# Mixture of experts, sorted on the chip by token count, every second expert in blocks of 64 tokens

## Chip, cores and metric

One core of a Trainium2 chip. The metric is the device time of one execution in microseconds, the median of several runs.

## The reference, cut to what matters

Two transformer blocks over 512 tokens of width 1024, all in float32. The change is in the second block's mixture of experts: 32 experts, each token goes to its four best.

```
logits = xt @ w_router + b_router
top_vals, top_idx = top_k(logits, 4);  gates = softmax(top_vals)
for each expert e, for the tokens xb that chose it:
    hgu = xb @ w_up_gate[e] + b_up_gate[e]            # 1024 -> 2048
    x_glu = min(hgu[:, :1024], 7);  x_lin = clip(hgu[:, 1024:], -7, 7)
    hact = x_glu * sigmoid(1.702 * x_glu) * (x_lin + 1)
    y = hact @ w_down[e] + b_down[e]                  # 1024 -> 1024
    out[token] += gate * y
```

`setup_inputs` draws fixed inputs, so each expert's count is fixed too.

## The kernel before

Float32 products are made of three passes over float32r parts: a value is split into a high part (ScalarE, L185) and a rest (VectorE, L188), and high x high, high x low and low x high are summed in PSUM (L165 issues every product).

The experts are a pipeline of steps (`moe`, L1769; `expert_step`, L1594). Step e runs, in 12 slots of one weight chunk (1 MB) each: four slots gate(e), four slots linear(e), four slots down(e-1). Each slot has 12 products of 128x128 by 128x512: two blocks of 128 rows of the weight, two PSUM banks, three parts. A block holds up to 128 tokens and is the stationary operand; the weights move. Beside the products stand, at fixed slots: evacuation and scatter of the outputs of e-2 (`evac`, L1641), transposes and split of the activations of e-1 (`tact`, `eact`), SiLU and clamp of e (`gate`, `act`), transposes and split of the gathered rows of e+1 (`tx`, `ex`), and the one-hot matrix, token table and row gather of e+2 (`gather_onehot`, `gather_table`, `gather_rows`, L1490 to L1538). Each engine works in the written order.

Weights come by SP's queue (`m_load`, L1547) in packets of 4 KB into 11 buffers of 1 MB (`mraw`), are split two chunks ahead (`m_ahead`, L1560, `m_la` = 2) into a ring of three hi/lo pairs (`mhl`, L1751), and PE releases a pair when its last product is done. PSUM is a rotation of eight banks (`ps`, L274 and L148). Bias rows enter as a first product of a selecting tile (`E4`) with all experts' biases (`BD`).

An expert with more than 128 tokens doesn't fit one block. Place 14 (`TWO`) has a second block in its step; `plan` finds on the chip the first expert from place 5 on that overflows and `swap` exchanges it with expert 14, before their weights are loaded by a run-time index (`order`). Blocks beyond that run in a loop after the steps (`tc.For_i`, L1854), each for itself. Every block runs the same instructions, whether it holds 16 tokens or 128.

The router (L1312) makes counts and ranks (`posm`), gates (`R`) and the first block before the steps begin.

Of the kernel before, what the change touches and what calls it, by code (L numbers as in the profile page):

```python
# [10 lines left out]
F32 = mybir.dt.float32  # L11
# [9 lines left out]
S = 512  # L21
D = 1024
# [6 lines left out]
TWO = 14  # L29
SWAP = 5  # L30
# [3 lines left out]
             ("cw2", 44), ("cb", 44), ("sbq", 1), ("sbk", 1), ("brt", 1),  # L34
             ("b_ada", 48)]
ROW_PARTS = [("mq_r", 32), ("mk_r", 32), ("rq", 64), ("rk", 64), ("gng", 512), ("gnb", 512)]
CST_PARTS = [("ident", 128), ("trin", 128), ("slow", 128), ("negm", 128), ("inv16", 16), ("inv32", 32),
             ("i32", 32), ("i128", 128), ("e4", 32), ("ule", 32), ("tok4", 4)]
# [12 lines left out]
COFF, CN = offsets(CST_PARTS)  # L51


def constants():
    p = np.arange(P)
    f = np.float32
    out = np.zeros((P, CN), f)

    def put(n, a):
        out[:, COFF[n][0]:COFF[n][1]] = a  # L60
# [9 lines left out]
    put("e4", (p[:, None] % 32) == np.arange(32)[None])  # L70
# [5 lines left out]
    return out, np.ascontiguousarray(dec.transpose(1, 0, 2))  # L76
# [7 lines left out]
def host_arrays(inp):  # L84
    g = {k: np.asarray(v) for k, v in inp.items()}
    one64 = np.ones(64, np.float32)
    one32 = np.ones(32, np.float32)
    cw = g["conv_w"].reshape(3, 2 * DFF)

    def hg(v):  # L90
# [10 lines left out]
        brt=np.concatenate([g["b_router_2"].reshape(-1), one32, one64])[:, None], b_ada=col(g["b_ada"]),  # L101
# [33 lines left out]
class Kernel:  # L135
# [25 lines left out]
    def cc(self, n):  # L161
        return self.cst[:, COFF[n][0]:COFF[n][1]]
# [1149 lines left out]
    def router(self, cr, right):  # L1312
# [41 lines left out]
        idf = rp.tile([P, NT, 4], F32, name="idf")  # L1354
        nc.vector.tensor_copy(idf, i8[:, :, 0:4])
        oh = rp.tile([P, NT * 4, NE], F32, name="oh")
        nc.vector.tensor_tensor(oh, idf.rearrange("p t r -> p (t r)")[:, :, None].to_broadcast([P, NT * 4, NE]),
                                self.cc("i32")[:, None, :].to_broadcast([P, NT * 4, NE]), op=OP.is_equal)
# [3 lines left out]
        nc.vector.memset(cm[:, 0, :], 0.0)  # L1362
        for t in range(NT):
            nc.vector.tensor_tensor(cm[:, t + 1, :], cm[:, t, :], M[:, t, :], op=OP.add)
        pp = self.ps()
        f = "p t e -> p (t e)"
        self.mm(pp[:, 0:NT * NE], self.cc("slow"), M.rearrange(f), True, False)
        self.mm(pp[:, 0:NT * NE], self.ones, cm[:, 0:NT, :].rearrange(f), False, True)
        pc = self.ps()
        self.mm(pc[0:NE, 0:1], cm[:, NT, :], self.ones[:, 0:1], True, True)  # L1370
        self.warm(10)
        pos = rp.tile([P, NT, NE], F32, name="pos")
        nc.vector.scalar_tensor_tensor(pos, pp[:, 0:NT * NE].rearrange("p (t e) -> p t e", e=NE), 1.0, M, op0=OP.add,
                                       op1=OP.mult)
        nc.vector.tensor_scalar(self.posm, pos, -1.0, 1.0, op0=OP.mult, op1=OP.add)
        nc.scalar.activation(self.cnt, pc[0:NE, 0:1], AF.Copy)
# [6 lines left out]
        for t in range(NT):  # L1383
# [10 lines left out]
        tmp = rp.tile([P, NT * 4, NE], F32, name="tmp")  # L1394
        nc.vector.tensor_tensor(tmp, oh, g4.rearrange("p t r -> p (t r)")[:, :, None].to_broadcast([P, NT * 4, NE]),
                                op=OP.mult)
        nc.vector.tensor_reduce(out=self.R[:, :, :, 1], in_=tmp.rearrange("p (t r) e -> p t e r", r=4), axis=AX.X,
                                op=OP.add)
# [4 lines left out]
    def overflow_blocks(self, rp):  # L1403

        nc = self.nc
        self.nb = nb = rp.tile([NE, 4], F32, name="nb")
        for b in range(3):
            nc.vector.tensor_scalar(nb[:, b:b + 1], self.cnt, 128.0 * (b + 1), None, op0=OP.is_gt)
        nc.vector.tensor_reduce(out=nb[:, 3:4], in_=nb[:, 0:3], axis=AX.X, op=OP.add)

    def plan(self, rp):


        nc, nb = self.nc, self.nb
        i32, jc = self.cc("i32")[0:16, :], self.cc("tok4")[0:16, 0:1]
        ci = rp.tile([16, NE], F32, name="ci")
        df = rp.tile([16, NE], F32, name="df")
        le = rp.tile([16, NE], F32, name="le")
        q = rp.tile([16, 4], F32, name="q")
        X = rp.tile([16, 4], F32, name="X")  # L1420
        ts, tt = nc.vector.tensor_scalar, nc.vector.tensor_tensor
        mx, has, two, dd = [q[:, k:k + 1] for k in range(4)]

        def place(out, e, t):
            ts(t, e, two, dd, op0=OP.is_equal, op1=OP.mult)
            tt(out, e, t, op=OP.add)
            ts(t, e, float(TWO), dd, op0=OP.is_equal, op1=OP.mult)
            tt(out, out, t, op=OP.subtract)

        pc = self.ps()  # L1430
        self.mm(pc[0:16, 0:NE], nb[:, 0:1].to_broadcast([NE, 16]), self.cc("ident")[0:NE, 0:NE], True, True)
        ts(le, i32, -1.0, float(2 * NE), op0=OP.mult, op1=OP.add)
        tt(le, le, pc[0:16, 0:NE], op=OP.mult)
        nc.vector.tensor_reduce(out=mx, in_=le[:, SWAP:NE], axis=AX.X, op=OP.max)
        yield
        ts(has, mx, 0.0, None, op0=OP.is_gt)
        ts(two, mx, -1.0, float(2 * NE - TWO), op0=OP.mult, op1=OP.add)
        tt(two, two, has, op=OP.mult)
        ts(dd, two, -1.0, None, op0=OP.mult)
        ts(two, two, float(TWO), None, op0=OP.add)  # L1440
        yield
        place(df, i32, le)
        nc.vector.tensor_copy(self.order[:, 0:NE], df[0:1, :])
        nc.vector.tensor_copy(self.order[:, NE:NE + 1], two[0:1, :])
        yield
        pc = self.ps()
        self.mm(pc[0:16, 0:NE], nb[:, 3:4].to_broadcast([NE, 16]), self.cc("ule")[0:NE, :], True, True)
        ts(le, i32, two, has, op0=OP.is_ge, op1=OP.mult)
        tt(ci, pc[0:16, 0:NE], le, op=OP.subtract)
# [4 lines left out]
        nc.vector.tensor_reduce(out=X[:, 0:1], in_=le, axis=AX.X, op=OP.add)  # L1454
        ts(X[:, 0:1], X[:, 0:1], float(NE - 1), None, op0=OP.min)
# [4 lines left out]
        ts(X[:, 2:3], X[:, 0:1], two, has, op0=OP.is_equal, op1=OP.mult)  # L1460
        tt(X[:, 1:2], X[:, 1:2], X[:, 2:3], op=OP.add)
        ts(X[:, 1:2], X[:, 1:2], 128.0, 128.0, op0=OP.mult, op1=OP.add)
        yield
        place(X[:, 3:4], X[:, 0:1], mx)
        nc.vector.tensor_copy(X[:, 2:3], ci[:, NE - 1:NE])
        Xi = rp.tile([16, 4], I32, name="Xi")
# [8 lines left out]
    def swap(self, rp):

        nc = self.nc
        e = nc.values_load(self.order[0:1, NE:NE + 1], engines=[mybir.EngineType.DVE], min_val=SWAP, max_val=NE - 1)
        def at(x):
            return (self.posm[:, :, x].rearrange("p t o -> p (t o)"),  # L1480
                    self.R[:, :, x, :].rearrange("p t o c -> p (t o) c"),
                    self.E4[:, :, x].rearrange("p i o -> p (i o)"))

        w = (rp.tile([P, NT], F32, name="sw0"), rp.tile([P, NT, 2], F32, name="sw1"), rp.tile([P, 2], F32R, name="sw2"))
        a, b = at(bass.ds(e, 1)), at(slice(TWO, TWO + 1))
        for to, fro in ((w, a), (a, b), (b, w)):
            for x, y in zip(to, fro):
                nc.vector.tensor_copy(x, y)

    def gather_onehot(self, d):  # L1490

        nc = self.nc
        oh = d["oh"] = self.mo.tile([P, NT, P], F32, name="ohp")
        for t in range(NT):
            nc.scalar.activation(oh[:, t, :], self.cc("i128"), AF.Abs, bias=d["pos"](t))
        oh = oh.rearrange("p t r -> p (t r)")
        nc.scalar.activation(oh, oh, AF.Relu, scale=-1.0, bias=1.0)
# [62 lines left out]
    def m_ahead(self):  # L1560
        while self.m_i < min(len(self.m_seq), self.m_done + 1 + self.m_la):
# [3 lines left out]
            self.split(raw, hi, lo)  # L1565
# [20 lines left out]
    def hl_tile(self, nm, d):  # L1586
# [4 lines left out]
        p = self.mx if nm == "x" else self.ml  # L1591
        return (p.tile([P, 8, P], F32R, name=nm + "h"), p.tile([P, 8, P], F32R, name=nm + "l"))

    def expert_step(self, cur=(), prev=(), pp=(), nxt=(), extra=None):  # L1594


        nc = self.nc
# [440 lines left out]
```

## Time and profile before

| | us |
|---|---|
| median of 3 runs | 2331.49 (2329.19 to 2333.32) |
| the profiled execution | 2335.76 |
| its span, first to last instruction | 2333.5 |
| PE / VectorE / ScalarE with work in the span | 2289.0 / 1748.6 / 1470.8 |

PE, DVE, ACT, POOL and SP are TensorE, VectorE, ScalarE, GpSimd and SyncE. A busy engine is one with an instruction in work; products are pipelined, so the start of one to the start of the next tells more than the length of one. "PEclk" is the clock granted to TensorE as a share of full speed, "DMA" the mean busy share of the 16 DMA engines. A wait is put down to the engine whose signal came last. Times in the rows count from the first instruction.

### The profile page before, as it was taken

How to read it: one execution, taken by the hardware profiler on the slowest of the kernel's cores; microseconds unless marked ns; L12 is line 12 of the kernel's file. 1: busy time of each engine (PE TensorE's matmuls, PEld its weight loads, DVE VectorE, ACT ScalarE, POOL GpSimd, SP SyncE). 2: the span in 40 equal slices, each digit the busy share in tenths (PEclk: the TensorE clock that was granted, in tenths of full speed). 3: DMA queues.
4: the chain of work that ended last, by engine and by line, in shares of the span. 5: the costliest groups of instructions: out<-in, count | busy, mean ns of one | idle time of the engine just before them, and what ended most of it. 6: DMA issues, size and time to landing. Idle time of an engine off the chain costs nothing. (4 is left out here: it accounts for less than half of the span.)

```text
span 2333.5 us, 29383 instructions
## 1 busy us (share of the span) xinstructions
PE 2289.0 (98%) x10792; PEld 1870.6 (80%) x10792; DVE 1748.6 (75%) x2138; ACT 1470.8 (63%) x1829; POOL 197.0 (8%) x108
## 2 busy tenths in 40 slices
PE   9999999999999999989999999999999999999988
PEld 8875688888888777777888888888888888888877
DVE  6877775566557367568988898867788889898963
ACT  3676543334444348556777878766687777877764
POOL 0100000000000000020011111200111011111100
PEclk8999999999999999999999999999999999999999
DMA  9240434333233122559999999987999999999861
GB/s 330 83 139 10 140 104 128 116 109 109 100 110 100 45 91 73 176 181 318 350 351 356 356 348 365 332 293 268 325 362 356 357 349 355 357 348 355 295 229 62
DMA packets 184611, 538.45 MB, mean 231 GB/s; under 512 B 16277, under 2 KB 41397, under 8 KB 184272
## 3 DMA queue, kind: packets, MB, share of 16 engines
q1 hardware_dynamic: 170128, 508.08, 60.9%
q0 software_dynamic: 11792, 26.12, 4.0%
q10 hardware_dynamic: 2544, 2.34, 0.3%
q8 instruction: 86, 1.41, 0.2%
q14 instruction: 61, 0.50, 0.1%
HBM read 530.47 MB, written 23.59 MB: 237 GB/s over the span
## 5 line engine op out<-in xcount | busy, mean ns | idle before, releaser
L188 DVE TENSOR_TENSOR mlo<-mraw,mhi 128x2048 fp32r<-128x2048 f32 x389 | 884.0, 2286 | 170.4 <-ACT mhi L185 151.3
L185 ACT ACTIVATE mhi<-mraw 128x2048 fp32r<-128x2048 f32 x389 | 741.5, 1914 | 283.3 <-PE ps L165 274.3
L165 PE MATMUL ps<-mhi,xh 128*128 128x512 f32 x1024 | 405.9, 396 | 0.0
L165 PE MATMUL ps<-mhi,xl 128*128 128x512 f32 x1024 | 401.2, 392 | 2.1 <-DVE xl L1581 2.1
L165 PE MATMUL ps<-mlo,xh 128*128 128x512 f32 x1024 | 274.1, 389 | 0.0
L188 DVE TENSOR_TENSOR wlo<-raw,whi 128x1024 fp32r<-128x1024 f32 (+2 forms) x128 | 153.1, 1207 | 112.4 <-ACT whi L185 112.2
L165 PEld LDWEIGHTS ps<-mhi,xl 128*128 128x128 f32 x1024 | 193.1, 189 | 42.3 <-DVE xl L1581 2.5
L165 PEld LDWEIGHTS ps<-mlo,xh 128*128 128x128 f32 x1024 | 192.2, 188 | 40.5
L165 PEld LDWEIGHTS ps<-mhi,xh 128*128 128x128 f32 x1024 | 192.9, 188 | 39.1 <-ACT xh L1580 0.2
L185 ACT ACTIVATE whi<-raw 128x1024 fp32r<-128x1024 f32 (+2 forms) x128 | 132.3, 1043 | 132.7 <-PE ps L165 131.3
L165 PE MATMUL ps<-mhi,ah 128*128 128x512 f32 x512 | 206.3, 403 | 0.3 <-ACT ah L1583 0.3
L165 PE MATMUL ps<-mhi,al 128*128 128x512 f32 x512 | 201.0, 393 | 0.2 <-DVE al L1584 0.2
L165 PE MATMUL ps<-whi,hh 128*128 128x512 f32 (+1 forms) x464 | 184.8, 398 | 5.5 <-ACT hh L185 2.4
L165 PE MATMUL ps<-wlo,hh 128*128 128x512 f32 (+1 forms) x464 | 181.6, 391 | 2.2 <-DVE wlo L188 2.2
L165 PE MATMUL ps<-whi,hl 128*128 128x512 f32 (+1 forms) x464 | 180.8, 390 | 0.0
L165 PE MATMUL ps<-mlo,ah 128*128 128x512 f32 x512 | 137.9, 391 | 0.0
L165 PE MATMUL ps<-hh,whi 128*128 128x512 f32 x352 | 137.8, 392 | 0.0
L1536 POOL DMA_INDIRECT xg<-hn_d,ix x31 | 72.6, 2343 | 769.9 <-PE ps L165 647.2
L165 PE MATMUL ps<-hh,wlo 128*128 128x512 f32 x352 | 137.0, 389 | 0.0
L165 PE MATMUL ps<-hl,whi 128*128 128x512 f32 x352 | 136.9, 389 | 0.0
L165 PEld LDWEIGHTS ps<-mlo,ah 128*128 128x128 f32 x512 | 96.1, 188 | 21.2
L165 PEld LDWEIGHTS ps<-mhi,ah 128*128 128x128 f32 x512 | 96.3, 188 | 20.1 <-ACT ah L1583 0.7
(487 smaller groups left out, 3660.1 us busy)
## 6 DMA issues: line engine op xcount, KB each, us to landing
mraw<-in_w_ug SPq DMA_DIRECT2D x256, 1024.0 KB, 7.8
mraw<-in_w_dn SPq DMA_DIRECT2D x128, 1024.0 KB, 7.5
raw<-in_w_up SPq DMA_DIRECT2D x44, 512.0 KB, 3.5
raw<-in_w_in SPq DMA_DIRECT2D x40, 512.0 KB, 3.7
wa<-in_w_ada SPq DMA_DIRECT2D x12, 1024.0 KB, 10.0
raw<-in_w_ada SPq DMA_DIRECT2D x24, 512.0 KB, 4.5
raw<-in_w_down SPq DMA_DIRECT2D x22, 512.0 KB, 3.5
raw<-in_w_out SPq DMA_DIRECT2D x16, 512.0 KB, 4.8
```

Source lines behind the costliest of these rows:

```text
L165: self.nc.tensor.matmul(out, l, r, start=start, stop=stop, skip_group_check=True)
L185: self.nc.scalar.activation(hi, raw, AF.Copy)
L188: self.nc.vector.tensor_tensor(lo, raw, hi, op=OP.subtract)
L1536: nc.gpsimd.indirect_dma_start(out=d["xg"], out_offset=None, in_=self.hn_d, in_offset=bass.IndirectOffsetOnAxis(ap=ix, axis=0), bounds_che ...
```

## The change

The ranks, gates and one-hot tables are made a second time after a sort: places 0 to 2 keep experts 0 to 2, the other 29 experts are ordered by count, and the upper 15 and the lower 14 take turns. The weights' run-time index starts at place 3. Place 3 (the largest count) has the second block. Places 4, 6, ... 30 are small: capacity 64. A small block's stationary tile has the high parts of its 64 tokens in columns 0 to 63 and the low parts in 64 to 127, so that two products (with the high and the low part of the weight) make all four terms; rows r and r + 64 of the result belong to one token. They are added for the activations by products with a matrix of two stacked identities (`sum2`), which also transpose, and for the outputs by scattering both halves with addition, one DMA each. Rows of a small block are gathered as two half rows, to partitions r and r + 64.

Gate and linear are no longer separate: one up chunk is 128 rows of the weight by all 2048 columns, with four PSUM banks open for eight slots. A down chunk gives partition p the rows 2p and 2p + 1. Both are 8 KB per partition in one piece. The columns of the activations are therefore read from PSUM at every second place (`pairs`). The first chunks are split in halves (`m_cut`). One tile `xg` instead of two holds gathered rows. The outputs of e-2 are evacuated ahead of the step's first product instead of behind it. The swap is gone, the plan of the overflow loop comes later and counts against each place's capacity.

```diff
-TWO = 14
-SWAP = 5
+FIRST = 3
+BIG = 15
+TWO = FIRST
+SMALL = [p >= FIRST and (p - FIRST) % 2 == 1 for p in range(NE)]
+CAP = [256 if p == TWO else 64 if SMALL[p] else 128 for p in range(NE)]
...
+    def sort(self, rp):
+        ts(kc, self.cnt, 32.0, self.cc("key")[0:NE], op0=OP.mult, op1=OP.add)
+        ps = self.ps()
+        self.mm(ps[0:NE, 0:NE], kc.to_broadcast([NE, NE]), ident, True, True)
+        ts(G, ps[0:NE, 0:NE], kc, None, op0=OP.is_lt)
+        yield
...
+        self.choices(oh)
+        yield
+        tt(tmp, oh, pl[:, None, :].to_broadcast([P, NT * 4, NE]), op=OP.mult)
...
+        pp, pc = self.ranks(rp, M, cm)
+        self.set_ranks(pp, pc, t[:, 3 * NT * NE:4 * NT * NE].rearrange("p (t e) -> p t e", e=NE), M)
+        yield
+        self.gates(oh, tmp)
+        self.select(self.ob, self.cc("val"))
...
             hi, lo = [self.mhl.tile([P, 2 * D], F32R, name=n) for n in ("mhi", "mlo")]
-            self.split(raw, hi, lo)
+            n = 2 * D // self.m_cut
+            for c in range(self.m_cut):
+                cs = slice(c * n, (c + 1) * n)
+                self.split(raw[:, cs], hi[:, cs], lo[:, cs])
...
-                    mms(d, ((0, 0), (1, 0)), False)
+                    mms(d, 0, range(len(d[x])), False)
...
-                    mms(d, ((0, 1),), True)
+                    mms(d, 1, (0,), True)
...
+        def act(d):
+            if d.get("small"):
+                d["us"] = [self.ma.tile([P, D], F32, name="mg") for _ in range(2)]
+                for b in range(4):
+                    z = wide(d["us"][b // 2][:, b % 2 * 512:b % 2 * 512 + 512])
+                    if b % 2:
+                        nc.vector.tensor_copy(z, pairs(d.pop(("u", b))))
+                    else:
+                        nc.scalar.activation(z, pairs(d.pop(("u", b))), AF.Copy)
+                return
...
+            for r in (slice(0, 64), slice(64, P)) if d.get("small") else (slice(0, P),):
+                nc.gpsimd.indirect_dma_start(
...
+            ps = d["aps", b] = self.ps()
+            for k in range(8):
+                self.mm(ps[:, k * 64:k * 64 + 64], d["us"][b][:, k * P:(k + 1) * P], self.cc("sum2"), True, True)
...
+        slots = [((cur, "x", "u", 0, 4, c), no, no) for c in range(8)] + \
+                [((prev, "a", "d", 1, 2, c), no, no) for c in range(4)]
...
+        put(0, on(evac, pp))
+        put(1, on(tact, ta, 0), on(eact, ta, 0))
+        put(2, on(tact, ta, 1), on(eact, ta, 1))
+        put(8, on(gate, cur), on(act, cur))
+        put(9, on(tx, nxt, 0), on(ex, nxt, 0))
+        put(10, on(tx, nxt, 1), on(ex, nxt, 1))
...
-        for w, b in ((wu, 0), (wu, 1), (wd, 0)):
-            if w is not None:
-                s += [w[c * 256:(c + 1) * 256, b * D:(b + 1) * D].rearrange("(k p) n -> p k n", p=P) for c in range(4)]
+        if wu is not None:
+            s += [wu[c * P:(c + 1) * P, :].rearrange("(k p) n -> p k n", p=P) for c in range(8)]
+        if wd is not None:
+            s += [wd[c * 256:(c + 1) * 256, :].rearrange("(p k) n -> p k n", p=P) for c in range(4)]
```

## Rows read from the trace of the kernel before

**Rows 1.** The page, parts 1 and 2: busy us and share; busy tenths in 40 slices.
```profile
PE 2289.0 (98%) x10792; PEld 1870.6 (80%) x10792; DVE 1748.6 (75%) x2138; ACT 1470.8 (63%) x1829; POOL 197.0 (8%) x108
...
DMA  9240434333233122559999999987999999999861
```

**Rows 2.** Windows: us, then PE, PEld, DVE, ACT, POOL busy, PEclk, DMA share, GB/s.
```profile
1110.00:1500.00 390.00, 390.00 (x1846) 324.19 (x1845) 346.02 (x264) 305.28 (x270) 52.17 (x22) 1.00 0.98 355
...
1035.00:1040.00 5.00, 4.37 (x24) 3.47 (x23) 4.79 (x11) 4.32 (x7) 0.00 (x0) 1.00 0.58 199
...
1060.00:1065.00 5.00, 2.85 (x14) 2.13 (x13) 4.72 (x14) 2.88 (x3) 1.02 (x1) 0.86 0.91 333
```

**Rows 3.** Waits of the whole span: who waited for whom, us, times, longest us.
```profile
POOL xg L1536 <- PE ps L165: 647.2, 26, 31.0
...
ACT mhi L185 <- PE ps L165: 274.3, 303, 3.8
...
DVE mlo L188 <- DMA mraw<-in_w_ug: 17.0, 27, 1.3
```

**Rows 4.** Timeline of PE in one steady step: start us, length us, line, operation, tiles.
```profile
1704.39 0.63 PE L165 MATMUL ps<-BD,E 128*128 128x512 f32 x2
...
1707.62 0.39 PE L165 MATMUL ps<-mhi,xh 128*128 128x512 f32 x1
...
1710.34 0.39 PE L165 MATMUL ps<-mhi,xh 128*128 128x512 f32 x1
...
1719.00 0.95 PE L165 MATMUL ps<-R,ohp 128*128 128x2 f32 x8
1719.80 0.64 PE L181 MATMUL ps<-cst,xg 128*128 128x128 f32 x4
...
1720.19 0.48 PE L165 MATMUL ps<-mhi,ah 128*128 128x512 f32 x1
...
1741.31 0.63 PE L165 MATMUL ps<-BD,E 128*128 128x512 f32 x2
```

**Rows 5.** Scatters of L1645 on POOL: count, ns min/median/max, first and last start.
```profile
L1645 POOL DMA_INDIRECT x_d<-my,ix x33: 1552/2391/3457, 1104.2 to 2258.5; - x33
```

**Rows 6.** Timeline of PE where the expert stage begins, fp32 products and a wait.
```profile
1026.35 0.61 PE L165 MATMUL ps<-ohp,hn 128*128 128x128 f32 x4
...
1027.24 0.61 PE L165 MATMUL ps<-ohp,hn 128*128 128x128 f32 x4
...
1063.77 0.79 PE L165 MATMUL ps<-mhi,xl 128*128 128x512 f32 x1 [2.15 <-DVE xl L1581]
1064.36 0.63 PE L165 MATMUL ps<-mhi,xh 128*128 128x512 f32 x1
1064.79 0.63 PE L165 MATMUL ps<-mhi,xl 128*128 128x512 f32 x1
```

**Rows 7.** Timeline of DVE in the same steady step.
```profile
1724.67 0.68 DVE L1581 TENSOR_TENSOR xl<-ps,xh 128x512 fp32r<-128x512 f32 x1
1725.28 2.28 DVE L188 TENSOR_TENSOR mlo<-mraw,mhi 128x2048 fp32r<-128x2048 f32 x1
1727.47 0.68 DVE L1581 TENSOR_TENSOR xl<-ps,xh 128x512 fp32r<-128x512 f32 x1
```

**Rows 8.** Groups of instructions by line: the evacuation, busy us and mean ns.
```profile
L1644 ACT ACTIVATE my<-ps,tb 128x512 f32<-128x512 f32 x66 | 41.1, 675 | 5.7 <-PE ps L165 5.7
```

**Rows 9.** DMA view, 1618 to 1640 us: GB/s in 40 slices, packets.
```profile
GB/s 380 425 424 425 410 432 410 424 410 432 402 410 402 417 395 417 410 410 402 387 410 410 395 313 395 410 417 417 410 417 387 417 402 410 402 402 380 372 305 268
DMA packets 2280, 8.78 MB, mean 399 GB/s; under 512 B 140, under 2 KB 140, under 8 KB 2279
```

**Rows 10.** DMA view, 1110 to 1500 us: queue of gathers and scatters, share of 16 engines.
```profile
q0 software_dynamic: 3168, 5.50, 5.4%
```

**Rows 11.** The page, part 6: DMA issues, count, KB each, median us to landing.
```profile
mraw<-in_w_ug SPq DMA_DIRECT2D x256, 1024.0 KB, 7.8
```

More of the change, by code (lines that the diff above doesn't have):

```diff
@@ L51 @@
 COFF, CN = offsets(CST_PARTS)
+MOFF, MN = offsets(MOE_PARTS)
 def constants():
@@ L1361, in router @@
         cm = rp.tile([P, NT + 1, NE], F32, name="cm")
[L1362 to L1370, printed above, removed]
-        self.warm(10)
[L1372 to L1376, printed above, removed]
+        pp, pc = self.ranks(rp, M, cm)
+        self.warm(10)
+        self.set_ranks(pp, pc, rp.tile([P, NT, NE], F32, name="pos"), M)
         d = self.ex[0]
@@ L1393, in router @@
         nc.vector.tensor_tensor(g4, g4, gs[:, :, None].to_broadcast([P, NT, 4]), op=OP.mult)
[L1394 to L1398, printed above, removed]
+        self.gates(oh, rp.tile([P, NT * 4, NE], F32, name="tmp"))
         self.m_la = 2
@@ L1401, in router, with ranks @@
         cx.close()
-    def overflow_blocks(self, rp):
+    def ranks(self, pool, M, cm):
         nc = self.nc
[L1406 to L1409, printed above, removed]
-    def plan(self, rp):
[L1414 to L1420, printed above, removed]
-        ts, tt = nc.vector.tensor_scalar, nc.vector.tensor_tensor
[L1422 to L1444, printed above, removed]
@@ new lines, in ranks @@
+        nc.vector.memset(cm[:, 0, :], 0.0)
+        for t in range(NT):
+            nc.vector.tensor_tensor(cm[:, t + 1, :], cm[:, t, :], M[:, t, :], op=OP.add)
+        pp = self.ps()
+        f = "p t e -> p (t e)"
+        self.mm(pp[:, 0:NT * NE], self.cc("slow"), M.rearrange(f), True, False)
+        self.mm(pp[:, 0:NT * NE], self.ones, cm[:, 0:NT, :].rearrange(f), False, True)
+        pc = self.ps()
+        self.mm(pc[0:NE, 0:1], cm[:, NT, :], self.ones[:, 0:1], True, True)
+        return pp, pc
@@ new lines, in gates, with select @@
+    def gates(self, oh, tmp):
+        nc = self.nc
+        nc.vector.tensor_tensor(tmp, oh, self.g4.rearrange("p t r -> p (t r)")[:, :, None]
+                                .to_broadcast([P, NT * 4, NE]), op=OP.mult)
+        nc.vector.tensor_reduce(out=self.R[:, :, :, 1], in_=tmp.rearrange("p (t r) e -> p t e r", r=4), axis=AX.X,
+                                op=OP.add)
+    def select(self, ids, val):
+        nc = self.nc
+        for i in range(2):
+            nc.vector.tensor_scalar(self.E4[:, i, :], ids, self.cc("mod"), self.cc("half")[:, i:i + 1],
+                                    op0=OP.is_equal, op1=OP.mult)
+            if val is not None:
+                nc.vector.tensor_tensor(self.E4[:, i, :], self.E4[:, i, :], val, op=OP.mult)
@@ new lines, in sort @@
+    def sort(self, rp):
+        nc = self.nc
+        ts, tt = nc.vector.tensor_scalar, nc.vector.tensor_tensor
+        ident, i32 = self.cc("ident")[0:NE, 0:NE], self.cc("i32")
+        kc = rp.tile([NE, 1], F32, name="kc")
+        G = rp.tile([NE, NE], F32, name="G")
+        ra = rp.tile([P, NE], F32, name="ra")
+        pl = rp.tile([P, NE], F32, name="pl")
+        self.ob = rp.tile([P, NE], F32, name="ob")
+        big = self.ma.tile([P, D], F32, name="mg")
+        oh, tmp = [big[:, 512 * i:512 * i + 512].rearrange("p (a b) -> p a b", b=NE) for i in range(2)]
+        ts(kc, self.cnt, 32.0, self.cc("key")[0:NE], op0=OP.mult, op1=OP.add)
[3 more added lines that the diff above has]
+        yield
+        ps = self.ps()
+        self.mm(ps[:, 0:NE], self.ones[0:NE, :], G, True, True)
+        ts(pl, ps[:, 0:NE], float(FIRST), 0.0, op0=OP.subtract, op1=OP.max)
+        ts(ra, ps[:, 0:NE], float(FIRST + BIG), 1.0 - 2 * BIG, op0=OP.is_ge, op1=OP.mult)
+        tt(pl, pl, ps[:, 0:NE], op=OP.add)
+        tt(pl, pl, ra, op=OP.add)
+        ts(G, pl[0:NE], self.cc("tok4")[0:NE, 0:1], None, op0=OP.is_equal)
+        tt(G, G, i32[0:NE], op=OP.mult)
+        nc.vector.tensor_reduce(out=kc, in_=G, axis=AX.X, op=OP.add)
+        yield
+        ps = self.ps()
+        self.mm(ps[:, 0:NE], kc.to_broadcast([NE, P]), ident, True, True)
+        nc.vector.tensor_copy(self.order, ps[0:1, 0:NE])
+        nc.vector.tensor_copy(self.ob, ps[:, 0:NE])
+        self.choices(oh)
+        yield
+        tt(tmp, oh, pl[:, None, :].to_broadcast([P, NT * 4, NE]), op=OP.mult)
+        nc.vector.tensor_reduce(out=self.idf.rearrange("p t r -> p (t r)"), in_=tmp, axis=AX.X, op=OP.add)
+        yield
+        self.choices(oh)
+        t = big[:, 512:D]
+        M, cm = t[:, 0:NT * NE].rearrange("p (t e) -> p t e", e=NE), \
+            t[:, NT * NE:(2 * NT + 1) * NE].rearrange("p (t e) -> p t e", e=NE)
+        nc.vector.tensor_reduce(out=M, in_=oh.rearrange("p (t r) e -> p t e r", r=4), axis=AX.X, op=OP.add)
+        yield
+        pp, pc = self.ranks(rp, M, cm)
+        self.set_ranks(pp, pc, t[:, 3 * NT * NE:4 * NT * NE].rearrange("p (t e) -> p t e", e=NE), M)
+        yield
+        self.gates(oh, tmp)
+        self.select(self.ob, self.cc("val"))
+        yield
@@ L1471, in plan @@
         nc.gpsimd.dma_start(self.ext, self.xi_d.rearrange("j c -> (j c)")[None, :])
-        nc.gpsimd.dma_start(self.extb, bass.AP(tensor=self.xf_d.tensor, offset=self.xf_d.offset, ap=[[0, P], [1, 16]]))
+        nc.gpsimd.dma_start(self.extb, bass.AP(tensor=self.xf_d.tensor, offset=self.xf_d.offset, ap=[[0, P], [1, NE]]))
         yield
[L1475 to L1488, printed above, removed]
     def gather_onehot(self, d):
@@ L1494, in gather_onehot @@
         for t in range(NT):
-            nc.scalar.activation(oh[:, t, :], self.cc("i128"), AF.Abs, bias=d["pos"](t))
+            nc.scalar.activation(oh[:, t, :], self.cc("i64" if d.get("small") else "i128"), AF.Abs, bias=d["pos"](t))
         oh = oh.rearrange("p t r -> p (t r)")
@@ L1591, in hl_tile, with expert_step @@
         p = self.mx if nm == "x" else self.ml
-        return (p.tile([P, 8, P], F32R, name=nm + "h"), p.tile([P, 8, P], F32R, name=nm + "l"))
-    def expert_step(self, cur=(), prev=(), pp=(), nxt=(), extra=None):
+        return [p.tile([P, 8, P], F32R, name=nm + n) for n in ("h" if d.get("small") else "hl")]
+    def expert_step(self, cur=(), prev=(), pp=(), nxt=(), extra=None, early=False):
         nc = self.nc
@@ L1606, in products, with mms @@
             w = []
-            def mms(d, parts, last):
-                for k2 in range(2):
-                    k = 2 * c + k2
-                    for b in range(2):
-                        for l, r in parts:
+            def mms(d, r, ls, last):
+                for k2 in range(4 // n):
+                    k = 4 // n * c + k2
+                    for b in range(n):
+                        for l in ls:
                             self.mm(d[out, b], d[x][l][:, k, :], w[r][:, k2, b * 512:(b + 1) * 512], False,
@@ new lines, in clamp @@
+        def clamp(l, ps):
+            nc.vector.tensor_scalar(l, ps, 8.0, -6.0, op0=OP.min, op1=OP.max)
+        def act(d):
+            if d.get("small"):
+                d["us"] = [self.ma.tile([P, D], F32, name="mg") for _ in range(2)]
+                for b in range(4):
+                    z = wide(d["us"][b // 2][:, b % 2 * 512:b % 2 * 512 + 512])
[3 more added lines that the diff above has]
+                        nc.scalar.activation(z, pairs(d.pop(("u", b))), AF.Copy)
+                return
+            for b in range(2):
+                l = self.ma1.tile([P, 512], F32, name="ml")
+                clamp(wide(l), pairs(d.pop(("u", 2 + b))))
+                mul(d["g"][:, b * 512:(b + 1) * 512], l)
@@ new lines, in eact @@
+        def eact(d, b):
+            ps = d.pop(("aps", b))
+            if not d.get("small"):
+                if b == 0:
+                    d["a"] = self.hl_tile("a", d)
+                self.half_evac(ps, d["a"], b, 1 / al)
+                return
+            if b == 0:
+                d["g"] = self.ma1.tile([P, 512], F32, name="mt")
+                nc.scalar.activation(d["g"], ps, AF.Silu, scale=al)
+                return
+            l = self.ma1.tile([P, 512], F32, name="ml")
+            clamp(l, ps)
+            mul(d["g"], l)
+            d["a"] = self.hl_tile("a", d)
+            g = d["g"].rearrange("p (k r) -> p k r", r=64)
+            h, lo = d["a"][0][:, :, 0:64], d["a"][0][:, :, 64:P]
+            nc.scalar.activation(h, g, AF.Copy, scale=1 / al)
+            nc.vector.scalar_tensor_tensor(lo, g, 1 / al, h, op0=OP.mult, op1=OP.subtract)
@@ L1657, in tx @@
         def tx(d, b):
-            d["xps"] = self.half_T(d["xg"][:, b * 512:(b + 1) * 512])
+            if b == 0 or not d.get("small"):
+                d["xps"] = self.half_T(d["xg"][:, b * 512:(b + 1) * 512])
         def ex(d, b):
@@ L1819, in moe @@
                 extra[2][0].append(table(ex[1]))
+                for i in range(2, 8):
+                    extra[i][1].append(lambda: next(sort))
+            if e == 1:
+                self.m_cut = 1
+                extra[0][1].append(lambda: next(sort))
+                extra[4][1].append(lambda: nc.vector.tensor_scalar(pcx, self.posm[:, :, TWO], 128.0, None, op0=OP.add))
             if e + 2 < NE:
-                extra[2][1].append(onehot(ex[e + 2]))
-                extra[4 if e + 2 == TWO else 9][0].append(table(ex[e + 2]))
+                extra[5][1].append(onehot(ex[e + 2]))
+                extra[10][1].append(table(ex[e + 2]))
             if e + 2 == TWO:
-                extra[5][1].append(onehot(second))
-                extra[9][0].append(table(second))
-            if e == 1:
-                self.overflow_blocks(m1)
+                extra[10][1].append(onehot(second))
+                extra[11][1].append(table(second))
+            if e == NE - 8:
                 plan = self.plan(m1)
-            if e == 2 or e == NE - 8:
-                for i in (0, 2, 4, 6, 8)[:3 if e == 2 else 5]:
+                for i in (0, 2, 4, 6, 8):
                     extra[i][1].append(lambda: next(plan))
-            if e == 3:
-                self.swap(m1)
-                nc.vector.tensor_scalar(pcx, self.posm[:, :, TWO], 128.0, None, op0=OP.add)
-            if SWAP - 1 <= e < NE:
-                wd = weights(place)[1] if e >= SWAP else A["w_dn"][e]
+            if FIRST - 1 <= e < NE:
+                wd = weights(place)[1] if e >= FIRST else A["w_dn"][e]
                 wu = None
```

214 lines of the change are left out of this document (123 added, 91 removed).

## The prediction

> **What bounds the kernel now.** The page first [rows 1]: TensorE (PE) shows work in 98% of the span, VectorE (DVE) in 75%, and the DMA row stands at 9 in nearly all of slices 19 to 37 of 40, the expert stage. The stage by windows [rows 2]: from 1110 to 1500 us PE is busy all of the time at full clock, DVE 346 of 390 us (89%), ScalarE (ACT) 305, the DMA engines 98% at 355 GB/s. Three resources are within 11% of full, so I read the waits [rows 3] to see which one the others wait for: ACT's first half of the weight split (L185) waits 274 us for PE, whose products release the three hi/lo buffers; DVE's second half (L188) waits 17 us in total for weights from w_ug; PE's waits are too short to be listed. PE sets the pace, and DVE and DMA stand close behind. That is the whole question: how far PE can be relieved before one of them takes over.
>
> One expert step, from the same bias product to the next, takes 1741.31 - 1704.39 = 36.92 us [rows 4]. A chunk of 12 products takes 2.72 us (1707.62 to 1710.34), 0.2267 us each; 144 of them are 32.6 us. The token table takes 0.80 us (1719.00 to 1719.80), four transposes 0.39 (to 1720.19), 16 of them 1.6. Bias products and changes between kinds make up the rest, 1.9 us.
>
> **The change, part by part.** The 2048 choices of the reference's inputs fall on the 32 experts as 198, 114, 104, 101, 81 and downwards. Sorted behind the first three, the 14 small places get 61 to 16 tokens, all within 64, and only the 198 exceeds 128, which the double place holds. L1645 scatters 33 times [rows 5], 32 experts and one second block: the overflow loop ran no time before and should run no time after.
>
> *PE.* A small expert drops one product of three: 64 instead of 96 up, 32 instead of 48 down. Step e holds up(e) and down(e-1), so in steps 4 to 31 small steps (small up, big down) have 112 products and big steps 128. Added in a big step: the small block's activations are summed and transposed by 16 fp32 products, two passes each; eight such passes with 128 columns take 1027.24 - 1026.35 = 0.89 us [rows 6], so 32 passes 3.6 us. With 64 columns they could be as cheap as the 0.10 us of a transpose [rows 4], 3.1 us; I take 3.6, the same kind of product. Big step: 29.0 + 1.9 + 0.8 + 0.4 + 3.6 = 35.7 us. Small step: 25.4 + 1.9 + 0.8 + 1.6 = 29.7 us. A pair costs PE 65.4 instead of 73.8 us.
>
> *DVE.* Splits in succession start 2.19 us apart with one 512-column operation taking 0.61 of its own (1724.67, 1725.28, 1727.47 [rows 7]); one that waits for the one before takes its 0.68. Big step: 12 splits 26.3, clamps and multiplies 2.7, the small block's clamp, multiply and low part 2.0, one x part 0.6, small ones 0.7: 32.3. Small step: 26.3, two copies of the small block's sums 1.3, two a parts and two x parts 2.4, 0.6: 30.6. Pair: 62.9 us, below PE's 65.4 but not evenly: only two chunks can be split ahead (three buffers, one in use), 4.4 us of lead. By portions, PE against DVE: up of a small step 16.3 / 18.7, down in it 13.2 / 11.9, up of a big step 26.5 / 19.5, down in it 9.2 / 12.8. The last portion eats 3.6 of the lead, the next needs 2.4 and finds 0.8: PE waits 1.6 us. The new order also puts the evacuation of the previous outputs (L1644) ahead of the next step's first product; with eight PSUM banks in rotation the fourth bias product of a big step needs a bank that it frees. One evacuation takes 0.68 us [rows 8]; between none and two of them with PE idle, I take 0.5. Pair: 67.5 us. The copies and clamps now read PSUM with a stride of two; no row shows such a read. Bounds: nothing, or twice the time, 4 x 0.61 = 2.4 us of DVE per pair; I take nothing, the rows of the same operations, and keep the end.
>
> *ACT* was busy 305 of 390 us [rows 2], 28.9 us of a step, and gets no more to do: covered by PE's 32.7.
>
> *DMA.* Bytes per expert stay at 12.58 MB. Where transfers had piled up behind the double step the queue moved 399 GB/s for 22 us with hardly any gather or scatter in it [rows 9]: 31.5 us per expert. Gathers and scatters take 5.4% of the engines' time [rows 10], 2.0 us of a step: 33.5. At the mean of the stage, 355 GB/s at 98%, a step of 36.9 us holds 36.2 us. So 33.5 to 36.2 per step; packets of 8 KB instead of 4 can move either end, and no row has enough of them to say by how much. I take 34.4, nearer to the piled-up row, since after the change transfers wait in the queue as they did there: 68.8 per pair, and it, not PE's 67.5, ends the pair, at **69.0** with what little PE and DMA don't overlap.
>
> The Trainium skill (page "DMA: Bandwidth & Descriptors", section "Where 436 GB/s comes from") says that for transfers between HBM and SBUF the HBM side binds at about 358 GB/s per core; by it an expert takes an estimated 35.1 us before gathers, and the sum comes to that of the first rival. The trace differs: 399 GB/s [rows 9].
>
> *The sort.* It runs in step 0 and the start of step 1: some 8 operations of 512 columns and 25 small ones, about 9 us of DVE, where DVE has 4 us free per step [rows 2]. In three places a PE product waits for a DVE result that is queued behind a split; each costs at most a split and the operations before it, about 3 us, none if DVE is ahead: 0 to 15 us in all, I take 6. The removed swap and part of the old plan ran on DVE's free time: nothing. Moving the second block from place 14 to 3 keeps its products; in step 3 it takes all eight PSUM banks, so the evacuations before and after stand on the path: 0 to 8 us, I take 3.
>
> *POOL and SP.* Fourteen small blocks scatter twice, the second waiting until the first has landed; behind it stands the next gather, which today waits 647 us in 26 times for PE [rows 3], 25 us each: covered. One xg tile instead of two: the next gather follows the transposes that read it, a step ahead of its use. Two more place loads on SP come while weights lie ready: covered; without that cover each would add its own microsecond. The smaller first splits change nothing that lasts.
>
> **Sum.** Fourteen pairs: 14 x (73.8 - 69.0) = -67; sort +6, double step +3: -58 us. The profiled execution took 2335.8 us (span 2333.5), 4.3 above the median of the runs, 2331.5. So 2277.8 for such an execution, **2273.5** as a median.
>
> **Rivals.**
> - *DMA is full already*: the 98% are capacity, not demand; a step can't go below 36.2 less what 8 KB packets save, say 35.8. For it: 355 GB/s is the level of the whole stage. Against: the 399 GB/s. 14 x 2.2 = 31, less 9: 2309.
> - *Everything overlaps*: PE's 65.4 is reached, packets of 8 KB bring DMA below it. For it: bins up to 432 GB/s [rows 9]. 14 x 8.4 = 118, less 9: 2222.
> - *Slower: the clock falls in the up half of small steps.* There PE waits for splits in every chunk. After the wait of 2.15 us at 1063.77 products came 0.43 us apart (1064.36, 1064.79 [rows 6]), half speed, with a mean granted clock of 0.86 in that window [rows 2]. If all 64 products of a small up ran so, PE would need 65.4 + 64 x 0.20 = 78.4 per pair: 14 x 4.6 + 9 = +73, 2405. It decides for slower from some 20 slow products per pair (58 us of gain over 14 pairs are 4.1 us). Against: the waits are about half a microsecond per chunk, and from 1035 to 1040, with 0.63 us idle, the clock stayed at 1.00 [rows 2].
> - *It doesn't do what it says*: routing on the chip differs and a small place overflows. A pass of the loop has 12 transfers of 7.8 us [rows 11] through two buffers, 47 us, with its start some 55: 2329, no change.
>
> **How the numbers follow.** Forecast 0.47 (its own range 2252 to 2296: DVE's and DMA's bounds, sort and double step), DMA full 0.22, overlap 0.20, slower 0.07, overflow 0.04. The range reaches to the second and third cases: 2220 to 2316. 0.2% is 4.7 us, about what a measurement tells from no change. Faster: 0.47 + 0.20 + 0.21 of the DMA case = 0.88; same 0.04; slower 0.08, the clock and a piece of the others.
>
> **What would show it.** Bias products of equal places a pair apart: 69 us (65 to 72 are the rivals). Groups of products with xl and al only in big steps, 16 fp32 products on us. DVE over 91% in the stage, DMA rate near 380 GB/s, and waits of DVE or ACT for w_ug well above 17 us if DMA binds, PE waiting for mlo in small up halves if DVE does. Step 0 longer by some 6 us. A granted clock below 1.00 in the stage, a scatter count above 33 + 14 = 47, or a pair above 73.8 us would prove the forecast wrong.

## The result and the profile after

The changed kernel takes 2303.63 us (median, 2299.9 to 2305.95) against 2332.05 for the kernel before in the same session: a ratio of 0.9878, 95% interval 0.9861 to 0.9896. It is faster by 28 us where 58 were forecast; the direction was right, the size less than half; the time lies inside the range of 2220 to 2316. The profiled execution took 2305.09 us with a span of 2303.3, 30.2 below the span of before.

The page of the changed kernel, parts 1 and 2, and the scatters from its groups of instructions by line; they answer to [rows 1, 5]:

```profile
PE 2204.6 (96%) x10410; PEld 1775.0 (77%) x10410; DVE 1731.2 (75%) x2178; ACT 1450.1 (63%) x1830; POOL 242.8 (11%) x121
...
DMA  9240333343233122356859999999999999999851
...
L1728 POOL DMA_INDIRECT x_d<-my,ix x47 | 127.7, 2716 | 180.4 <-DMA x_d<-my,ix 99.6 <-ACT my L1726 65.7 <-DVE mlo L200 6.5
```

PE's busy time fell by 84 us, the time by 30. The 47 scatters are 33 + 14: no small place overflowed. Where did the rest go? The starts of PE's bias products of one pair, a big step and a small one (timeline of PE, answers to [rows 4]; columns as there):

```profile
1396.83 0.40 PE L177 MATMUL ps<-BD,E 128*128 128x512 f32 x1
...
1434.01 0.40 PE L177 MATMUL ps<-BD,E 128*128 128x512 f32 x1
...
1467.37 0.40 PE L177 MATMUL ps<-BD,E 128*128 128x512 f32 x1
```

A big step takes 37.18 us, a small one 33.36, the pair 70.5 where 73.8 stood before and 69.0 were forecast. (All steps below are such distances.) The two steps as windows (columns as in [rows 2]):

```profile
1396.83:1434.01 37.18, 35.83 (x180) 29.95 (x178) 30.21 (x20) 27.79 (x25) 5.95 (x2) 1.00 0.96 373
1434.01:1467.40 33.39, 31.54 (x144) 24.11 (x143) 33.18 (x29) 28.08 (x26) 7.08 (x3) 1.00 0.98 383
```

The clock is full. In the big step DVE has 7.0 us free and PE waits 1.35; in the small step it has 0.2 us free and PE waits 1.85. The sum of DVE per pair, 63.4 us, looks harmless beside 70.6, but it is not spread evenly. The waits of the changed kernel from 1400 to 1800 us say for whom (answers to [rows 3]; PEld is TensorE's load of a product's stationary operand):

```profile
PEld ps L177 <- DVE mlo L200: 36.5, 45, 1.8
...
DVE mlo L200 <- ACT mhi L197: 35.2, 29, 1.9
...
ACT ah L1757 <- DVE mt L1703: 22.1, 6, 3.7
PE ps L177 <- DVE mlo L200: 18.1, 23, 1.4
...
DVE mlo L200 <- DMA mraw<-in_w_ug: 1.1, 1, 1.1
```

PE waits for low parts (`mlo`), of which the list of the kernel before shows nothing from 1110 to 1500 us, and in 400 us one split waited 1.1 us for weights. The place is seen in the timelines of the same pair, first DVE, then ACT, then PE:

```profile
1422.18 2.28 DVE L200 TENSOR_TENSOR mlo<-mraw,mhi 128x2048 fp32r<-128x2048 f32 x1
1425.64 2.29 DVE L200 TENSOR_TENSOR mlo<-mraw,mhi 128x2048 fp32r<-128x2048 f32 x1 [1.18 <-ACT mhi L197]
1427.85 0.68 DVE L1706 TENSOR_SCALAR ml<-ps 128x512 f32<-128x512 f32 x1
...
1430.63 2.29 DVE L200 TENSOR_TENSOR mlo<-mraw,mhi 128x2048 fp32r<-128x2048 f32 x1
...
1422.72 1.09 ACT L1700 ACTIVATE mg<-ps 128x512 f32<-128x512 f32 x2 [0.98 <-PE ps L177]
1423.69 3.72 ACT L197 ACTIVATE mhi<-mraw 128x2048 fp32r<-128x2048 f32 x2
...
1423.20 0.63 PE L177 MATMUL ps<-BD,E 128*128 128x512 f32 x2
...
1426.87 1.07 PE L177 MATMUL ps<-mlo,ah 128*128 128x512 f32 x4
...
1429.52 1.18 PE L177 MATMUL ps<-mlo,ah 128*128 128x512 f32 x4
...
1432.97 0.50 PE L177 MATMUL ps<-mlo,ah 128*128 128x512 f32 x1 [1.35 <-DVE mlo L200]
```

PE ends the up half at 1423.2, which frees a hi/lo pair; ACT makes the next high part from 1423.69 on, and DVE, which had nothing to do for 1.18 us, the low part from 1425.64 to 1427.93. PE uses it at 1429.52, only 1.6 us later. Then four clamps and multiplications stand ahead of the next split, and PE waits 1.35 us. From 1427.85 to 1469.37 DVE has no gap, and up to 1453 PE or its load waits in nearly every chunk.

### The profile page after: what moved, and what is told of

It reads as the page before. It is cut to its first block, busy times and chain, and to the rows that moved or that the text cites. A ratio compares the mean times of both kernels' runs of the same rounds, so it can differ in the third digit from the quotient of the medians.

```text
span 2303.3 us, 28759 instructions
## 1 busy us (share of the span) xinstructions
PE 2204.6 (96%) x10410; PEld 1775.0 (77%) x10410; DVE 1731.2 (75%) x2178; ACT 1450.1 (63%) x1830; POOL 242.8 (11%) x121
## 3 DMA queue, kind: packets, MB, share of 16 engines
q8 instruction: 83, 1.36, 0.2%
## 5 line engine op out<-in xcount | busy, mean ns | idle before, releaser
L200 DVE TENSOR_TENSOR mlo<-mraw,mhi 128x2048 fp32r<-128x2048 f32 (+1 forms) x403 | 875.8, 2209 | 141.9 <-ACT mhi L197 133.4
L197 ACT ACTIVATE mhi<-mraw 128x2048 fp32r<-128x2048 f32 (+1 forms) x403 | 732.1, 1852 | 121.1 <-PE ps L177 111.1
L177 PE MATMUL ps<-mhi,xh 128*128 128x512 f32 x1024 | 351.7, 397 | 0.0
L177 PE MATMUL ps<-mlo,xh 128*128 128x512 f32 x1024 | 286.7, 402 | 28.8 <-DVE mlo L200 26.6
L177 PEld LDWEIGHTS ps<-mlo,xh 128*128 128x128 f32 x1024 | 184.8, 188 | 100.7 <-DVE mlo L200 66.7
L177 PE MATMUL ps<-mhi,xl 128*128 128x512 f32 x576 | 225.1, 391 | 0.0
L177 PE MATMUL ps<-mhi,ah 128*128 128x512 f32 x512 | 178.6, 402 | 0.0
L1728 POOL DMA_INDIRECT x_d<-my,ix x47 | 127.7, 2716 | 180.4 <-DMA x_d<-my,ix 99.6
L177 PEld LDWEIGHTS ps<-mhi,xl 128*128 128x128 f32 x576 | 108.6, 188 | 22.1
L177 PE MATMUL ps<-mhi,al 128*128 128x512 f32 x288 | 114.0, 396 | 1.1 <-DVE al L1641 1.1
```

Of the source, the lines that this page charges most:

```text
L177: self.nc.tensor.matmul(out, l, r, start=start, stop=stop, skip_group_check=True)
L197: self.nc.scalar.activation(hi, raw, AF.Copy)
L200: self.nc.vector.tensor_tensor(lo, raw, hi, op=OP.subtract)
L1728: nc.gpsimd.indirect_dma_start(out=self.x_d, out_offset=bass.IndirectOffsetOnAxis(ap=d["ix"][0:r.stop - r.start, 0:1], axis=0), in_=d["y"][r],
```

## The experiments

Three theories. **L**, short lead: DVE idles in a big step because a ring of three hi/lo pairs lets it be only two chunks ahead, and is behind from the end of that step through the small one. **M**: the memory rate sets the pair. **A**: ACT's waits in its written order hold back the high parts. Each run has a ratio to the kernel before with its interval.

### Four hi/lo pairs: `ring4`

```diff
-        self.mrawA = self.pool("mrawa", 5, ctx=cx, side="right")
+        self.mrawA = self.pool("mrawa", 3, ctx=cx, side="right")
-        self.mhl = self.pool("mhl", 3, ctx=cx, side="right")
+        self.mhl = self.pool("mhl", 4, ctx=cx, side="right")
-        self.m_la = 2
+        self.m_la = 3
```

(Besides, two tiles behind the steps are taken from other pools.)

> Edit: four hi/lo pairs instead of three and splits three chunks ahead, paid for with two of the eleven weight buffers. Theory L (short lead): VectorE idles some 6 us of a big step because it may be only two chunks ahead, and has no gap from the end of that step through the small step, where TensorE waits 3.4 us per pair for low parts. With one chunk more of lead the pair should fall from 70.6 to about 68 (67 to 69.2), 14 x 2.6 = 36 us: 2268 (2255 to 2285). Rival M (the memory rate sets the pair): nothing gained, with two buffers fewer 2304 to 2320. Rival A (ScalarE's waits in its written order hold back the high parts): part of the gain, 2285 to 2304.

Measured: 2269.42 us, 0.9731 (0.9715 to 0.9747); steps 35.5 and 32.8, pair 68.3. Its window and waits from 1400 to 1800 us:

```profile
1400.00:1800.00 400.00, 390.25 (x1867) 316.52 (x1867) 369.77 (x273) 328.51 (x289) 67.44 (x28) 1.00 0.99 387
```

```profile
PEld ps L177 <- DVE mlo L200: 19.7, 25, 1.1
...
PE ps L177 <- DVE mlo L200: 8.2, 12, 0.7
```

PE's wait for low parts fell from 18.1 to 8.2 us and that of its loads, which overlaps it, from 36.5 to 19.7; ACT's wait of 22.1 us for the multiplication stayed, so it isn't what cost these 2.2 us per pair of steps. Four hi/lo pairs with all eleven weight buffers weren't tried.

### Half of the bytes: `halfload`

```diff
+        if k < 4 and self.m_i >= 48:
+            self.nc.sync.dma_start(t[:, 0:D], src[:, 0, 0:D])
+            return t[:, None, 0:D].to_broadcast([P, 2, D])
```

> Leaves out half of every weight transfer from chunk 48 on (each split reads the loaded half twice), all else as it is. Theory L and rival A: no engine waits for weights, so the pair stays at 70.6 and the time at 2304 (2298 to 2307). Rival M: the transfers of a pair fall from about 70 to about 38 us, the pair to what TensorE and VectorE allow, 67 to 69: 2260 to 2282.

Measured: 2304.24 us, 0.9878 (0.9861 to 0.9894); steps 37.2 and 33.4. The window of 1400 to 1800 us, with nearly half the rate (373 GB/s in the changed kernel) and PE, DVE and ACT within 0.3 us of what they were busy:

```profile
1400.00:1800.00 400.00, 381.01 (x1817) 306.11 (x1816) 357.82 (x265) 316.23 (x277) 72.18 (x29) 1.00 0.63 196
```

Theory M falls. That its price in the prediction, 2309, was the nearest of all to the result is a coincidence.

### The same VectorE work at two places: `dve_small`, `dve_big`

```diff
                 self.half_evac(ps, d["a"], b, 1 / al)
+                if d["place"] >= FIRST and not d.get("second"):
+                    v = [z[:, b * 4:b * 4 + 4, :].rearrange("p a b -> p (a b)") for z in d["a"]]
+                    nc.vector.scalar_tensor_tensor(v[1], ps, 1 / al, v[0], op0=OP.mult, op1=OP.subtract)
```

> Adds two VectorE operations per pair in the small step: the low part of a big block's activations is made twice, 2 x 0.68 = 1.36 us, in the stretch in which VectorE has no gap. Theory L: they stand on the path with nearly their whole length, pair 71.9, 14 x 1.3 = 18: 2322 (2316 to 2325). Rival M: hidden, 2304. Rival A: hidden in ScalarE's waits, 2304 to 2309.

```diff
             clamp(l, ps)
+            clamp(l, ps)
+            clamp(l, ps)
             mul(d["g"], l)
```

> Adds the same 1.36 us of VectorE per pair in the big step, between the small block's clamp and multiplication, where VectorE has gaps; ScalarE's wait for that multiplication grows from 3.7 to 5.1 us. Theory L: hidden, at most 0.3 us per pair: 2304 (2301 to 2309). Rival A: the high parts come 1.4 us later and the pair is as much longer: 2318 to 2323. Rival M: 2304.

Measured: `dve_small` 2322.66 us, 0.9958 (0.9946 to 0.997), small step 34.8 instead of 33.4; `dve_big` 2303.18, 0.9881 (0.9865 to 0.9898), steps 37.2 and 33.4. In the small step 1.36 us of DVE cost 1.4, in the big step nothing, although ACT's wait there rose to 5.1 us (30.8 us in six times). That settles L against A.

### The change without its small blocks: `no_small`

```diff
-SMALL = [p >= FIRST and (p - FIRST) % 2 == 1 for p in range(NE)]
+SMALL = [False] * NE
```

> Keeps everything of the change (sort, order of the chunks, 8 KB pieces, reads at every second place, evacuation ahead, double step at place 3) but the blocks of 64: all places are full. Theory L: nothing of the rest costs or gives anything in a steady step, which is set by TensorE as before, 36.9 us (36.7 to 37.1); the early steps cost what they cost in the changed kernel, +7 to +12: 2332 + 9 = 2341 (2337 to 2346). Rival S (the strided reads, the evacuation ahead of the products or the 8 KB pieces change a step by themselves): a step other than 36.9 by 0.3 us or more, 8 us in the time.

Measured: 2342.87 us, 1.0054 (1.0035 to 1.0072); every steady step 36.9. The strided reads, the evacuation ahead and the 8 KB pieces together change nothing in a steady step that PE sets; what they cost DVE or the queue beneath that, this run can't show. The first five steps take 223.5 us, 9 more than the same kinds of steps before. The rest of the 13 us between the medians has no place in the profiled executions, whose spans differ by 6.2.

### The sort: `no_sort`, `sort_spread`

`no_sort` fills `order` with 0 to 31, makes no tables a second time and plans no overflow.

> Leaves the sort out: the order is 0 to 31, the small places compute only the first 64 of their tokens and no overflow is planned. Theory L: the sort is what lengthens step 0 from 27 to 37 us (TensorE waits 1.6 and 2.5 us for VectorE, then runs at half clock): step 0 at 27 to 30, 2295 (2291 to 2299). Rival: step 0 is longer for the new chunk order, the sort is covered: 2302 to 2306.

```diff
         ts(kc, self.cnt, 32.0, self.cc("key")[0:NE], op0=OP.mult, op1=OP.add)
+        yield
...
-        pp, pc = self.ranks(rp, M, cm)
+        self.sums(M, cm)
+        yield
+        pp, pc = self.ranks(rp, M, cm, False)
...
-                for i in range(2, 8):
+                for i in (2, 3, 4, 5, 6):
...
-                extra[0][1].append(lambda: next(sort))
+                for i in (0, 1, 2, 3):
+                    extra[i][1].append(lambda: next(sort))
```

> The same sort, in nine pieces over steps 0 and 1 instead of seven in step 0, with each product of TensorE a slot behind the VectorE work that it needs. Theory L with the clock: the waits of 1.6 and 2.5 us in step 0 and the half clock behind the second go, VectorE's work stays: step 0 at 30 to 33 us, step 1 at 38 to 41, 2299 (2295 to 2302). Rival: VectorE's sum counts in these steps, and only what TensorE's waits hide differs: 2302 to 2306.

Measured: `no_sort` 2293.46 us, 0.9835 (0.9816 to 0.9853), step 0 at 26.8 instead of 37.1; `sort_spread` 2296.58, 0.9848 (0.983 to 0.9866), step 0 at 28.3 (below the 30 to 33 expected), step 1 at 40.8 instead of 39.4. So the sort costs 10 us where it stands and 3 where PE need not wait for it. The changed kernel's windows show how, PE idle for 2.1 of 3 us and then at half clock (0.50, 1.2 GHz) for 7 us:

```profile
1064.00:1067.00 3.00, 0.94 (x5) 0.70 (x5) 2.20 (x8) 0.00 (x0) 0.00 (x0) 0.67 0.68 243
1067.00:1074.00 7.00, 7.00 (x26) 6.12 (x26) 5.33 (x13) 4.24 (x6) 0.00 (x0) 0.50 0.34 140
```

### Both: `ring4_spread`

> Four hi/lo pairs (nine weight buffers) and the spread sort together. Theory L: the two gains add, being in different steps: 2269 - 5 = 2264 (2260 to 2268). Rival: four pairs already cover the sort's waits, 2267 to 2271.

Measured: 2264.63 us, 0.9717 (0.97 to 0.9734), pair 68.3. The gains add: the first five steps take 7.1 us less than in `ring4` (221.08 to 214.01), where the spread sort alone took off 7.2 (220.45 to 213.22). This version beats both kernels, the one before by 65 us (2329.58 in its session).

### Less work for VectorE: `pool_mul`, `ring4_spread_pool`, `best_half`, `no_mul`

```diff
-                mul(d["g"][:, b * 512:(b + 1) * 512], l)
+                g = d["g"][:, b * 512:(b + 1) * 512]
+                nc.gpsimd.tensor_scalar(g, g, top, None, op0=OP.min)
+                nc.gpsimd.tensor_tensor(g, g, l, op=OP.mult)
```

> On the changed kernel: GpSimd instead of VectorE multiplies a big block's two halves (as a minimum and a product), which takes 2 x 0.69 us per pair out of VectorE's stretch without gaps. Theory L: TensorE's waits fall by nearly as much, pair 69.2 (69.0 to 69.8), 14 x 1.35 = 19: 2285 (2281 to 2291). Rival M: 2304. Rival P (GpSimd's operations, some 1.2 us each behind the clamps, come too late for TensorE's transposes in the small step): 2304 or more.

> Four pairs, spread sort and GpSimd's multiplication together. Theory L: of the 3 us by which the pair of 68.3 stands above TensorE's own 65.2, 1.3 go: pair 67.0 (66.6 to 67.6), 2265 - 18 = 2247 (2243 to 2254). Rival M (at 387 GB/s and 99% the memory rate is now the bound): pair 68, 2260 to 2265, with waits for weights in the list.

> The same with half of every weight transfer left out from chunk 48 on. Theory L: as ring4_spread_pool within 3 us. Rival M: faster than it by 5 to 25 us.

Measured: `pool_mul` 2301.27 us, 0.9867 (0.9843 to 0.9891), steps 36.4 and 34.1, pair 70.5; `ring4_spread_pool` 2264.34, 0.9709 (0.9686 to 0.9733), pair 68.2; `best_half` 2265.24, 0.9714 (0.9691 to 0.9738). Theory L missed by 16 us in the first and 17 in the second. The second lies at theory M's price, but halving the bytes again changed nothing, at 389 GB/s without it. Nor does rival P explain the first: in its list of waits from 1400 to 1800 us PE waits for low parts alone, never for a tile of POOL. The timeline of `pool_mul`, DVE and then POOL:

```profile
1429.63 3.06 DVE L200 TENSOR_TENSOR mlo<-mraw,mhi 128x2048 fp32r<-128x2048 f32 x1
1432.62 0.68 DVE L1775 TENSOR_TENSOR xh<-ps,xh 128x512 fp32r<-128x512 f32 x1
1433.22 2.28 DVE L200 TENSOR_TENSOR mlo<-mraw,mhi 128x2048 fp32r<-128x2048 f32 x1
...
1435.78 0.89 DVE L1573 SCALAR_TENSOR_TENSOR tb<-tb 128x1 f32<-128x1 f32 x1
...
1429.27 1.28 POOL L1723 TENSOR_TENSOR mg<-mg,ml 128x512 f32<-128x512 f32 x1 [2.86 <-DVE ml L1706]
1430.63 3.41 POOL L1722 TENSOR_SCALAR mg<-mg 128x512 f32<-128x512 f32 x1
1434.12 2.53 POOL L1723 TENSOR_TENSOR mg<-mg,mt 128x512 f32<-128x512 f32 x1
```

DVE's split beside POOL's first multiplication takes 3.06 instead of 2.28 us, and a one-column operation 0.89 instead of 0.16, ending with POOL's second: 1.5 us lost for 2 x 0.69 removed. The last run takes the multiplication away without POOL:

```diff
-                mul(d["g"][:, b * 512:(b + 1) * 512], l)
+                if d["place"] <= FIRST:
+                    mul(d["g"][:, b * 512:(b + 1) * 512], l)
```

> Leaves out VectorE's multiplication of gate and linear half of the big blocks from place 4 on (2 x 0.69 us per pair), without GpSimd. Theory L, with the two operations of GpSimd as what gave the gain back in pool_mul (VectorE's split beside them took 3.06 instead of 2.28 us): pair 69.2 (69.0 to 69.8), 13.5 x 1.35 = 18: 2285 (2281 to 2291). Rival (less work of VectorE at this place shortens nothing): pair 70.4 and 2300 or more, as in pool_mul.

Measured: 2280.08 us, 0.9778 (0.9759 to 0.9798); steps 35.7 and 33.4, pair 69.1, as theory L had it; the time is a little under its range.

## Why the prediction was wrong

The step that failed is "Pair: 67.5 us" and the 69.0 that followed: "only two chunks can be split ahead ..., 4.4 us of lead", of which "the last portion eats 3.6 ..., the next needs 2.4 and finds 0.8: PE waits 1.6 us". The place was right: DVE runs short of lead from the end of a big step into the small one. The lead was mis-sized, and the DMA queue, which was to end the pair at 69.0, ended none. The lead was counted as two splits of DVE. But a hi/lo pair that PE frees is first filled by ACT (1.86 us) and only then by DVE (2.29), in series. In the timeline DVE has no work for 1.18 us right before the tight stretch, and its low part is ready 1.6 us ahead of use, not 4.4. Of the 6.0 us that the two portions need, most is then paid by PE: the pair stands 5.1 us above PE's forecast 65.4, where 2.1 were reckoned. `ring4` gives back 2.2, `no_mul` 1.4, and 1.36 us more of DVE cost 1.4. The result lies in the range only because the range reaches to the rival with a full DMA queue, which isn't what happened; the forecast's own 2252 to 2296 misses it.

What PE pays is seen in a chunk of the small step, from its timeline:

```profile
1444.10 1.08 PE L177 MATMUL ps<-mhi,xh 128*128 128x512 f32 x4
1445.86 1.20 PE L177 MATMUL ps<-mlo,xh 128*128 128x512 f32 x4 [0.69 <-DVE mlo L200]
1446.89 1.08 PE L177 MATMUL ps<-mhi,xh 128*128 128x512 f32 x4
```

Behind four products 0.23 us apart the next could start at 1445.01; it starts 0.85 later, and the four with `mlo` take 1.03 us instead of 0.91. Such lateness adds up to 1.7 us in the big step and 3.55 in the small one, 5.3 per pair, more than the idleness that the windows record. Four hi/lo pairs don't take all of it away (`ring4_spread`, columns as in [rows 2]):

```profile
1384.67:1420.22 35.55, 35.55 (x179) 30.04 (x178) 30.59 (x25) 27.80 (x25) 4.77 (x2) 1.00 1.01 401
1420.22:1453.02 32.80, 31.26 (x144) 24.22 (x143) 32.70 (x24) 28.04 (x26) 7.26 (x3) 1.00 0.98 377
```

The big step has no wait left. The small one, in which DVE is busy for 32.7 of 32.8 us, still holds 2.65 us of lateness.

Point by point:

- *PE's own work, 65.4 per pair*: it held: 35.45 and 29.8 without lateness, where 35.7 and 29.7 were forecast (its portions of the small step, 16.3 and 13.2, make 29.5).
- *DVE, 62.9 per pair*: 63.4. The strided reads at nothing: right, a clamp that reads every second column takes 0.69 us in the mean (L1706), as the clamp of the kernel before did.
- *Evacuation ahead, 0.5*: nothing. The four bias products of the big step start 0.23 us apart from 1396.83 on, and the next product follows at 1397.76.
- *ACT covered*: right, even with a wait of 5.1 us (`dve_big`).
- *DMA ends the pair, 69.0*: wrong. A pair of 70.5 comes out with half of the bytes too; the queue had room to the 387 GB/s of `ring4`, where nobody waits for it either. So the first rival falls. The Trainium skill (page "DMA: Bandwidth & Descriptors", section "Where 436 GB/s comes from") has HBM bind at about 358 GB/s per core; the 387 GB/s over 400 us here are above that, and the measurement decides. (With the forecast's 2.0 us of gathers beside it, that figure makes an estimated 37.1 us a step and no gain, not the first rival's 35.8.)
- *Sort +6, double step +3*: the sort is 10 (within its 0 to 15), nearly all in step 0, where PE waited for inputs of the sort's products and then ran at half clock. The double step at place 3 and the next one take 59.2 and 49.2 in `no_small`, against 59.7 and 49.2 at places 14 and 15 before: nothing. The first five steps took 220.5 us; before, steps 0 to 2 with 14 and 15 took 214.4. That is +6.1, against +9 less half a pair's gain, +6.6.
- *POOL and SP*: covered. The second scatters waited 99.6 us in 14 times for the first, and the next gather still waits for PE. A place load would not have cost a microsecond: it occupies SP for about 0.45 us (L1951).
- *The slower rival*: the clock stayed at 1.00 in the steady steps, with PE waiting in every small step. *Overflow*: none; no run entered the loop, so its price, the 8 us for its start above all, stays unshown.

The sum: 27 steps from place 5 on took 957.4 us for 996.6 (before, steps 3 and 4 counted for 14 and 15), -39.2, where 13.5 x 4.8 = 65 were forecast; the first five +6.1; the stage began 1.6 later, and what follows the last step took 1.3 longer. Together -30.2. Of the 28 us that are missing, 26 are the pairs' (2.3 of these in the one small step that carries the plan, 35.7 us); what follows the last step varied from 83 to 92 us between the profiled executions of all runs, which stays unexplained.

## What to carry to other kernels

The lead that a ring of buffers gives is the time from a buffer's release to its use, less what the engines that fill it take one after the other; count that, not the number of buffers. Where two kinds of step take turns, compare the engines stretch by stretch: an engine that is free by 10% over the pair can bind for half of it, while it idles in the other half because it may not run ahead. And buffers for which nobody waits (here two of eleven for weights) are worth more as depth where somebody does.

## What the hardware showed

- *VectorE and GpSimd hold each other up.* In `pool_mul` DVE's operations with both operands in SBUF were held until about the end of POOL's (1430.55 and 1436.65), and POOL's minimum ran 3.41 us, to 1.35 behind the end of DVE's split at 1432.69; the operation that reads PSUM kept its 0.68. The Trainium skill (page "SBUF — State Buffer", section "SBUF: two separate sides") says that the two share a pair of ports as an exclusive lock for a whole instruction; the trace agrees, with 1.5 us per pair.
- *The same wait doesn't always cost the clock.* In the changed kernel PE's wait of 2.50 us before 1066 was followed by a granted clock of 0.50 and products 0.43 us apart; in `dve_big` the same code waited 2.50 us from 1062 on and kept 1.00, and step 0 took 34.3 instead of 37.1 us:

```profile
1063.00:1066.00 3.00, 1.36 (x7) 1.11 (x8) 2.20 (x8) 0.41 (x2) 0.00 (x0) 1.00 0.65 205
1066.00:1069.00 3.00, 3.00 (x23) 2.66 (x21) 2.48 (x4) 2.96 (x5) 0.00 (x0) 1.00 0.69 289
```
